# A two-group encoder layer on one core: the order of TensorE and SP in the two attention stages written out by hand, transposes placed between wide products, the scaling of P moved to GpSimd

## The chip, the cores and the metric

The kernel runs on one core of a Trainium2 chip. The metric is the device time of one execution in microseconds (us). Lower is better. TensorE (PE in the views) multiplies, VectorE (DVE), ScalarE (ACT) and GpSimd (POOL) do elementwise work, and SyncE (SP) issues most of the loads from the chip's main memory (HBM). Each engine has its own queue of instructions, fixed when the kernel is built, and waits on semaphores.

## The reference

One encoder layer is applied with the same weights to two groups of tokens: a prompt of 512 and a sample of 1024, both 1024 channels wide, everything in float32. Cut to what matters:

```
u    = layer_norm(x) * (1 + sc1) + sh1          # sh, sc, g from silu(c) @ w_ada
qa, ka, va, qb, kb, vb, ga, gb = split(u @ w_in)
qa, ka = rope(rms_norm(qa)), rope(rms_norm(ka))
oa   = softmax(qa ka' / 8) va                   # global attention, 8 heads, 2 kv heads
ob   = softmax(qb kb' / 8 + bias) vb            # 8 heads, each token sees a window of 8 x 16 tokens
m    = (sigmoid(ga) * (oa @ w_out_a) + sigmoid(gb) * (ob @ w_out_b)) @ w_out
x    = layer_norm_affine(2**0.25 * x + (1 + g1) * m)
h    = square(relu((layer_norm(x) * (1 + sc2) + sh2) @ w_ff1)) @ w_ff2
y    = layer_norm_affine(2**0.25 * x + (1 + g2) * h)
```

## The kernel before

Tokens are handled in chunks of 512: the prompt is one, the sample two. A large product is made three times, with each operand split into a high part in the fast 32-bit format (fp32r) and the low rest (`whi` and `wlo` for weights): `mm3` issues high x high, high x low, low x high. Weights come in units of 128 x 1024 values: SP loads a unit into `wraw` (three buffers), ACT writes `whi` (L93), DVE `wlo` (L94), and `stream` does that one unit ahead of its use. A unit feeds 24 products 512 columns wide for a chunk.

The stages, with the times at which the trace shows them: the modulation and the prompt's projections (`proj`, to about 187 us), the prompt's gates (to 285), the prompt's attention together with the projections of both sample chunks (285 to 640), the sample's attention together with the sample's gates and then the prompt's merge (640 to 1138), the merges, output product and norms of the three chunks (to 1436), and the dense layers (to the end). In `proj` the order is q, then k and v of the global attention, then q and k of the local one, then its v.

An attention stage has a global part `gqa` and a local part `na`. In `gqa` a block is a kv head, a head and 512 queries; the prompt has 8 blocks, the sample 16. A step of a block is one tile of 128 queries: score products S of the tile with all keys (L534: two products for 512 keys, four for 1024), the maximum on DVE (L537), the exponential on ACT (L540), a reciprocal (L541), and the scaling of P, on ACT and DVE in turn (L543, L545). The values of the block before go on meanwhile: for each 128 keys four transposes of P into a PSUM tile T (L552), a split of T into `ph` and `pl` (L555, L556), and two products with V into the sums A (L565, L566). Scores have two PSUM buffers of one bank in the prompt, one of two banks in the sample. In `na` an item is a head, eight rows of the image and 16 columns, 32 items in the prompt and 64 in the sample: two score products over a window of 256 or 384 keys (L657), bias and maximum in one DVE instruction (L660), exponential (L664), scaling on DVE (L666), two or three transposes (L673), a copy on ACT (L675), and two or three value products (L680). `load` brings V of a pair of heads in 16 pieces (L619), then Q and K of the head (L622, L108), one head ahead; the bias tables come separately (L635).

What fills PE between the attention's steps is the other generator of the stage. `weave` runs generators side by side: each yields a number for its progress, and the one that is least far goes on. This gives a program order; a planner then orders the instructions of every engine anew by its own estimates of their times and by priority, SP's loads among them. The sample's merge (`out_merge`) loads gates (`og`), multiplies them with the products of oa and ob, adds the two on GpSimd (L755), and splits the sum.

```
        self.weave(attention(0), self.chain(*[(self.proj(c, U, tmp), 1) for c, U in zip(scs, US)]), finish())
...
        self.weave(attention(1), fill())
```

## Time and profile before

| | |
|---|---|
| median of 3 runs | 2508.99 us (2502.77 to 2511.89) |
| the profiled execution's own time | 2521.03 us |
| its span, first to last instruction | 2519.2 us |
| PE, matmuls | 2391.9 us busy, 95% of the span |
| PE, weight loads | 1902.1 us, 76% |
| DVE | 1475.1 us, 59% |
| ACT | 972.3 us, 39% |
| GpSimd | 472.6 us, 19% |
| mean granted clock of PE | 0.975 of 2.4 GHz |

The profile is of one execution. Matmuls are pipelined: a record begins before the one ahead of it has ended, so a busy PE is not PE at its peak, and the distance between the starts of two products says more than their lengths. The granted clock is the share of full speed that the chip allowed PE; its two levels are 1.2 and 2.4 GHz. The rows on which the prediction rests are in a section of their own, below.

### The profile page before, as it was taken

The page shows a single profiled execution, that of the slowest core. Times are in us where ns is not written, and L with a number is a line of the kernel's source. Part 1 is how long each engine was busy: PE and PEld are TensorE (multiplying, and loading weights), DVE is VectorE, ACT ScalarE, POOL GpSimd, SP SyncE. Part 2 cuts the span into 40 slices and gives each one's busy share as a digit, 9 for nine tenths or more (in the row PEclk, how much of TensorE's full clock was granted, in tenths as well). Part 3 has the DMA queues.
Part 4 walks back from the last instruction along what each step waited for, and adds up shares of the span by engine and source line. Part 5 has one row for each costly group of instructions (what it writes and reads, how often), then busy time and mean ns, then how long its engine had stood idle before and what let it go on. Part 6 is the DMA issues. An engine that isn't in the chain of part 4 may idle for free.

```text
span 2519.2 us, 29833 instructions
## 1 busy us (share of the span) xinstructions
PE 2391.9 (95%) x10992; PEld 1902.1 (76%) x10992; DVE 1475.1 (59%) x2511; ACT 972.3 (39%) x1589; POOL 472.6 (19%) x524
## 2 busy tenths in 40 slices
PE   5989999988999999999897999999999999999997
PEld 3867777766777777777776788887788888888876
DVE  6997686474677754675867754445733333333466
ACT  4434656434677754553434224232411211221222
POOL 4341242353000004431312000003100000000133
PEclk9999999988999999999998999999999999999999
DMA  6766634576112127766656524234511210211231
GB/s 248 251 222 221 213 130 155 144 196 217 63 53 76 49 69 198 183 188 195 194 199 206 169 76 154 96 97 127 177 34 42 67 42 26 67 50 34 68 117 59
DMA packets 124227, 325.85 MB, mean 129 GB/s; under 512 B 20240, under 2 KB 35632, under 8 KB 124080
## 3 DMA queue, kind: packets, MB, share of 16 engines
q1 hardware_dynamic: 105744, 266.21, 34.8%
q0 software_dynamic: 18048, 57.69, 6.5%
q8 instruction: 87, 1.43, 0.2%
q14 instruction: 60, 0.49, 0.1%
q10 hardware_dynamic: 288, 0.03, 0.0%
HBM read 261.99 MB, written 62.93 MB: 129 GB/s over the span
## 4 chain that ended last, share of the span: by engine, by line
PE 66%; DVE 11%; issue 8%; DMA 7%; POOL 4%; ACT 2%; SPq 0%; POOLq 0%; ACTq 0%; DVEq 0%
PE D L112 18%; PE D L114 18%; PE D L113 18%; PE S L534 3%; PE T L552 3%; PE A L680 2%; DVE wlo L94 2%; PE A L565 2%; PE A L566 1%; DMA wraw<-in_wst 1%; PE T L673 1%; POOL og L755 1%; PE S L657 1%; ACT whi L93 1%; DMA og<-g 1%
## 5 line engine op out<-in xcount | busy, mean ns | idle before, releaser
L93 ACT ACTIVATE whi<-wraw 128x1024 fp32r<-128x1024 f32 x266 | 279.1, 1056 | 846.2 <-PE D L114 423.8
L114 PE MATMUL D<-uh,wlo 128*128 128x512 f32 x1344 | 534.1, 397 | 10.2 <-DVE wlo L94 10.2
L112 PE MATMUL D<-uh,whi 128*128 128x512 f32 x1344 | 536.0, 399 | 3.9 <-DVE stk L341 1.9
L113 PE MATMUL D<-ul,whi 128*128 128x512 f32 x1344 | 532.7, 396 | 0.0
L94 DVE TENSOR_TENSOR wlo<-wraw,whi 128x1024 fp32r<-128x1024 f32 x266 | 333.1, 1255 | 317.8 <-ACT whi L93 316.9
L112 PE MATMUL D<-whi,hh 128*128 128x512 f32 x768 | 304.6, 398 | 7.5 <-ACT hh L863 7.5
L114 PEld LDWEIGHTS D<-uh,wlo 128*128 128x128 f32 x1344 | 255.3, 190 | 68.6 <-DVE wlo L94 13.1
L114 PE MATMUL D<-whi,hl 128*128 128x512 f32 x768 | 303.6, 397 | 0.7 <-DVE hl L864 0.6
L113 PE MATMUL D<-wlo,hh 128*128 128x512 f32 x768 | 303.3, 397 | 0.0
L112 PEld LDWEIGHTS D<-uh,whi 128*128 128x128 f32 x1344 | 255.5, 190 | 59.2 <-issue 3.0
L113 PEld LDWEIGHTS D<-ul,whi 128*128 128x128 f32 x1344 | 255.5, 190 | 53.7 <-issue 0.9
L885 DVE TENSOR_TENSOR y<-y,D 128x512 f32<-128x512 f32 x168 | 115.2, 686 | 214.6 <-PE D L114 214.0
L112 PEld LDWEIGHTS D<-whi,hh 128*128 128x128 f32 x768 | 145.4, 189 | 44.7 <-ACT hh L863 11.2
L114 PEld LDWEIGHTS D<-whi,hl 128*128 128x128 f32 x768 | 145.3, 190 | 36.9 <-DVE hl L864 3.1
L113 PEld LDWEIGHTS D<-wlo,hh 128*128 128x128 f32 x768 | 145.5, 189 | 33.6
L846 POOL TENSOR_TENSOR y<-y,g 128x1024 f32<-128x1024 f32 x12 | 28.8, 2400 | 754.0 <-DVE y L885 754.0
L537 DVE TENSOR_REDUCE m<-S 128x1 f32<-128x1024 f32 (+1 forms) x96 | 99.7, 1041 | 44.8 <-PE S L534 44.6
L112 PE MATMUL D<-whi,uh 128*128 128x512 f32 (+1 forms) x288 | 106.0, 370 | 13.9 <-DVE stk L341 8.2
L556 DVE TENSOR_TENSOR pl<-T,ph 128x512 fp32r<-128x512 f32 x160 | 107.0, 684 | 14.6 <-ACT ph L555 13.8
L555 ACT ACTIVATE ph<-T 128x512 fp32r<-128x512 f32 x160 | 93.4, 596 | 52.2 <-PE T L552 50.7
L113 PE MATMUL D<-wlo,uh 128*128 128x512 f32 (+1 forms) x288 | 105.5, 366 | 3.1 <-DVE wlo L94 3.0
L114 PE MATMUL D<-whi,ul 128*128 128x512 f32 (+1 forms) x288 | 105.0, 365 | 0.0
(170 smaller groups left out, 3845.7 us busy)
## 6 DMA issues: line engine op xcount, KB each, us to landing
wraw<-in_w SPq DMA_DIRECT2D x132, 512.0 KB
wraw<-in_wst SPq DMA_DIRECT2D x56, 512.0 KB
wraw<-in_wada SPq DMA_DIRECT2D x32, 512.0 KB
g<-gst POOLq DMA_DIRECT2D x48, 256.0 KB, 3.5
og<-g SPq DMA_DIRECT2D x48, 256.0 KB
wraw<-in_wab SPq DMA_DIRECT2D x24, 512.0 KB
wraw<-in_wo SPq DMA_DIRECT2D x24, 512.0 KB
raw<-in_wada_k SPq DMA_DIRECT2D x16, 512.0 KB
```

Of the source, the lines that this page charges most:

```text
L93: nc.scalar.activation(hi, raw, AF.Copy)
L94: (engine or nc.vector).tensor_tensor(lo, raw, hi, op=ALU.subtract)
L112: mm(out, l[0], r[0], start=start, stop=False)
L113: mm(out, l[0], r[1], start=False, stop=False)
L114: mm(out, l[1], r[0], start=False, stop=stop)
L534: nc.tensor.matmul(S[:, k * CH:(k + 1) * CH], q, K[r][:, k * CH:(k + 1) * CH], start=r == 0, stop=r == 1)
L537: nc.vector.tensor_reduce(m, S[:, :T], axis=AX.X, op=ALU.max, negate=True)
L552: nc.tensor.transpose(tp[:, qt * P:(qt + 1) * P], Ps[qt][:, k * P:(k + 1) * P], self.ident)
L555: nc.scalar.activation(ph, tp, AF.Copy)
L556: nc.vector.tensor_tensor(pl, tp, ph, op=ALU.subtract)
L565: nc.tensor.matmul(acc, V[:, k, :], ph, start=k == 0, stop=False)
L885: nc.vector.tensor_tensor(y[:, hs], y[:, hs], ps, op=ALU.add)
```

## The change

In the two attention stages PE's and SP's instructions keep the order in which the program issues them (`in_order`), so `weave` alone sets it; the other engines stay with the planner, and softmax, splits and the ends of blocks are issued at high priority. For that every generator goes on in small steps. `mm3s` yields after each product, and takes a waiting transpose of a projection (`small`) behind each. `gqa` issues a transpose and a wide product in turn, its transposes two steps (prompt: one) after the block's last softmax, its value products two groups (one) later. `na` runs transposes two items behind the scores and value products three behind. Each part lets the other generator lead at first (`LEAD`, `NLEAD`).

P is scaled on GpSimd for three tiles of a block and on ACT for the fourth. In the sample's `gqa` scores have two PSUM buffers of two banks and the fill one bank (`psD1`), with eight empty yields after each gate chunk (`GAP`); `na` gives the fill a second bank. K of `gqa` has two buffers. Weights of the sample's projections and of the gates are asked for two units ahead. `proj` makes the local v first and does its ropes and stacks in the eight units of the local q and k; the rows of gates (`mod_finish`) come in the middle of the first sample chunk, and their store goes to GpSimd's queue. In `out_merge` of the sample the low part of the weights is made on GpSimd and the two gated products are added on DVE. The diff, cut:

```diff
-GL = 0.06
 AHEAD = 1
-GQ = (0.55, 0.55)
-AT = (1.1, 0.94)
+GQ = (0.55, 0.66)
+AT = (1.02, 0.96)
+LEAD = (0.06, 0.12)
+NLEAD = (0.2, 0.26)
+GAP = 8
+HP = 1000
...
+    def in_order(self, *gens):
+
+        with self.tc.manual_schedule(engines={mybir.EngineType.PE, mybir.EngineType.SP}):
+            self.weave(*gens)
...
+    def mm3s(self, out, l, r, start, stop):
+
+        mm = self.nc.tensor.matmul
+        for i, (x, y) in enumerate(((l[0], r[0]), (l[0], r[1]), (l[1], r[0]))):
+            mm(out, x, y, start=start and i == 0, stop=stop and i == 2)
+            if self.small:
+                self.small.pop(0)()
+            yield
...
-        return self.psD.tile([P, CH], F32, tag="D", name="D")
+        self.nd += 1
+        return self.psD[self.nd % len(self.psD)].tile([P, CH], F32, tag="D", name="D")
...
+                self.small.extend([lambda: None] * 10 + [partial(row, s, gi, c0)])
...
+        self.small.extend(partial(turn, t) for t in range(TT))
...
+    def proj_weights(self, chunks):
+        a = self.a
+        return self.stream(([a["wvb"][i] for i in range(4)] + [a["wq"][i] for i in range(4)]
+                            + [a["wkv"][i] for i in range(2)] + [a["wst"][i] for i in range(8)]) * chunks,
+                           ahead=chunks)
...
-        todo = {2: [(q_rope, 0)], 3: [(q_rope, 1), (k_rope, 0)], 4: [(q_rope, 2), (k_rope, 1)],
-                5: [(q_rope, 3), (k_rope, 2)], 6: [(k_rope, 3)],
-                7: [(q_stack, 0)], 8: [(q_stack, 1)], 9: [(q_stack, 2)], 10: [(q_stack, 3)], 11: [(k_stack, 0)]}
+        todo = {1: [(q_rope, 0), (k_rope, 0)], 2: [(q_rope, 1), (k_rope, 1)], 3: [(q_rope, 2), (k_rope, 2)],
+                4: [(q_rope, 3), (k_rope, 3)], 5: [(k_stack, 0), (q_stack, 0)], 6: [(q_stack, 1), (q_stack, 2)],
+                7: [(q_stack, 3)]}
...
-            for (seq, t0), p in zip(chs, ps):
+        for i, w in enumerate(self.stream([a["wst"][8 + i] for i in range(16)], ahead=2)):
+            for (seq, t0), U in zip(chs, Us):
+                ps = []
+                yield from self.wstats(w, U, ps)
                 g = pool.tile([P, CH], F32, tag="gst", name="gst", bufs=2)
-                nc.scalar.activation(g, p, func)
+                nc.scalar.activation(g, ps[0], func)
                 nc.gpsimd.dma_start(self.scr[seq]["g"][i][:, t0:t0 + CH], g)
+                for _ in range(GAP if len(self.psD) == 1 else 0):
+                    yield
...
+        LAG, DEPTH = (2, 2) if nh > 1 else (1, 1)
...
+                    got.append(psp.tile([P, T], F32, tag="ST" if nh == 1 else "S", name="S", bufs=3 if nh == 1 else 2))
+                nc.tensor.matmul(got[0][:, k * CH:(k + 1) * CH], q, K[r][:, k * CH:(k + 1) * CH],
+                                 start=r == 0, stop=r == 1)
...
+                p = pool.tile([P, T], F32, tag="P", name="P", bufs=8 + LAG)
+                z = pool.tile([P, 1], F32, tag="z", name="z", bufs=4)
+                nc.scalar.activation(p, S[:, :T], AF.Exp, bias=m, scale=1.0, accum_out=z)
+                nc.vector.reciprocal(z, z)
+                if qt < TT - 1:
+                    nc.gpsimd.tensor_scalar(p, p, z, None, op0=ALU.mult)
+                else:
+                    nc.scalar.activation(p, p, AF.Copy, scale=z)
+                Ps[blk].append(p)
...
-            if qt % 2:
-                nc.vector.tensor_scalar(p, p, z, None, op0=ALU.mult)
-            else:
-                nc.scalar.activation(p, p, AF.Copy, scale=z)
...
+            return [partial(turn, qt) for qt in range(TT)], split
...
+        second = [None] * (TT + LAG) + [(b, k) for b in blocks for k in range(nk)]
+        second[:TT + LAG] = [None] * (kq * (TT + LAG))
+        steps = len(second) // kq + 1
...
+            for j in range(kq):
+                small, split = [], None
+                if kq * i + j < len(second) and second[kq * i + j]:
+                    small, split = turns(*second[kq * i + j])
+                big, end = bigs[j * 2:j * 2 + 2], None
+
+                hold = DEPTH + (pend[0][1] == 0) if pend else 0
+                n = len(pend) - DEPTH + 1 if small else 2
+                while pend and n > 0 and (len(pend) >= hold or not small):
+                    b, e = products()
+                    big, end, n = big + b, end or e, n - 1
+                for n in range(max(len(small), len(big))):
+                    for x in (small, big):
+                        if n < len(x):
+                            x[n]()
+                    yield lead + (1.0 - lead) * (i + (j + (n + 1.0) / TT) / kq) / (steps + 1)
+                with self.tc.high_priority(HP):
+                    if split:
+                        split()
+                    if end:
+                        finish(end)
+            if softmax:
+                with self.tc.high_priority(HP):
+                    softmax()
+        while pend:
...
+        lead = NLEAD[seq]
+        yield lead
+        n = len(items)
+        for i in range(n + 3):
...
+            big, softmax = scores(*items[i]) if i < n else ([], None)
+            small, copy = turns(ps.pop(0)) if 2 <= i < n + 2 else ([], None)
+            for j in range(max(len(big), len(small))):
+                for x in (big, small):
+                    if j < len(x):
+                        x[j]()
+                with self.tc.high_priority(HP):
+                    if softmax and j == 1:
+                        ps.append(softmax())
+                    if copy and j == ng - 1:
+                        pts.append(copy())
+                yield lead + (1.0 - lead) * (i + (j + 1.0) / (1 + ng)) / (n + 3)
+            if i >= 3:
+                it, pt = items[i - 3], pts.pop(0)
+                for g in range(ng):
+                    weigh(*it, pt, g)
+                yield lead + (1.0 - lead) * (i + 1.0) / (n + 3)
...
+        ws = self.primed(self.stream((a["wab"][n] for n in range(KT)), engine=nc.gpsimd if seq else nc.vector))
...
-            nc.gpsimd.tensor_tensor(ts[0], ts[0], ts[1], op=ALU.add)
+            (nc.vector if seq else nc.gpsimd).tensor_tensor(ts[0], ts[0], ts[1], op=ALU.add)
...
+                if seq and name == "g":
+                    p, more = psum("psDn", bufs=1)
+                    self.psD = self.psD + [p]
...
+        ws = self.proj_weights(2)
+        both = [(self.share(self.proj(c, U, tmp, ws, f), 488), 1)
+                for c, U, f in zip(scs, US, (partial(self.mod_finish, tmp), None))]
+        self.in_order(self.chain(*both), attention(0))
...
-        self.psD, psD_st = psum("psD3", bufs=3)
+        p, psD_st = psum("psD1", bufs=1)
+        self.psD = [p]
...
-            for x in self.gates(scs, US, tmp, AF.Copy):
+            for x in self.share(self.gates(scs, US, tmp, AF.Copy), 768 + 16):
...
-
-        self.weave(attention(1), fill())
+            merge = self.share(self.out_merge(pc, om["pool"], M), 200)
+            next(merge)
+            yield 0.86
+            for x in merge:
+                yield 0.86 + 0.14 * x
+
+        self.in_order(fill(), attention(1))
         psD_st.close()
```

## Rows read from the trace of the kernel before

**Rows 1.** Busy time by stage: us, engines (x instructions), clock, DMA share, GB/s.

```profile
285.00:478.00 193.00, 184.66 (x941) 150.06 (x941) 129.99 (x235) 113.16 (x216) 73.83 (x93) 0.98 0.45 141
478.00:640.00 162.00, 140.62 (x612) 104.19 (x613) 86.07 (x239) 60.01 (x140) 61.31 (x90) 0.85 0.66 195
640.00:931.00 291.00, 290.69 (x1471) 226.09 (x1469) 209.07 (x312) 210.13 (x331) 18.87 (x34) 1.00 0.18 55
931.00:1138.00 207.00, 200.88 (x1084) 153.57 (x1082) 118.29 (x374) 96.55 (x228) 82.59 (x97) 0.98 0.70 185
1138.00:1436.00 298.00, 276.07 (x1168) 220.41 (x1167) 206.13 (x294) 108.02 (x144) 57.26 (x50) 0.96 0.59 192
```

**Rows 2.** Timeline of PE, sample's gqa: start us, us, engine, line, operation.

```profile
706.62 0.39 PE L566 MATMUL A<-pl,V 128*128 128x512 f32 x1
706.85 0.27 PE L552 MATMUL T<-ident,P 128*128 128x128 f32 x1
706.88 1.18 PE L534 MATMUL S<-K,Q 128*128 128x512 f32 x4
707.89 0.49 PE L552 MATMUL T<-ident,P 128*128 128x128 f32 x3
...
708.45 0.39 PE L566 MATMUL A<-pl,V 128*128 128x512 f32 x1
708.69 0.60 PE L552 MATMUL T<-ident,P 128*128 128x128 f32 x4
709.07 0.49 PE L565 MATMUL A<-ph,V 128*128 128x512 f32 x1
709.41 0.39 PE L113 MATMUL D<-ul,whi 128*128 128x512 f32 x1
```

**Rows 3.** Timeline of PE in the sample's na.

```profile
1005.12 0.87 PE L680 MATMUL A<-pt,V 128*64 128x128 f32 x6
1005.92 0.55 PE L673 MATMUL T<-ident,P 128*128 128x128 f32 x3
```

**Rows 4.** Waits of PE, 478 to 640: us in total, times, longest.

```profile
PE D L112 <- DVE stk L341: 6.5, 1, 6.5
PE S L657 <- DMA K<-kb: 5.8, 2, 4.0
PE S L657 <- DVE m L660: 5.6, 4, 2.1
```

**Rows 5.** Timeline of SP's issues, na of prompt and sample.

```profile
481.11 16.06 SPq L619 DMA_DIRECT2D V<-vb  x16
...
497.83 3.05 SPq L108 DMA_DIRECT2D K<-kb  x4
...
954.13 24.83 SPq L619 DMA_DIRECT2D V<-vb  x16
```

**Rows 6.** Groups by line and form: busy us, mean ns, idle before.

```profile
L537 DVE TENSOR_REDUCE m<-S 128x1 f32<-128x1024 f32 x64 | 78.0, 1219 | 25.4 <-PE S L534 25.4
...
L540 ACT ACTIVATE P<-S,m 128x1024 f32<-128x1024 f32 x64 | 71.4, 1115 | 14.6 <-DVE m L537 13.9
...
L545 ACT ACTIVATE P<-P,z 128x1024 f32<-128x1024 f32 x32 | 36.7, 1148 | 4.3 <-DVE z L541 4.3
...
L846 POOL TENSOR_TENSOR y<-y,g 128x1024 f32<-128x1024 f32 x12 | 28.8, 2400 | 754.0 <-DVE y L885 754.0
...
L497 ACT ACTIVATE gst<-D 128x512 f32<-128x512 f32 x48 | 28.3, 589 | 44.3 <-PE D L114 24.7 <-DMA g<-gst 10.9 <-issue 8.6
...
L543 DVE TENSOR_SCALAR P<-P,z 128x1024 f32<-128x1024 f32 x32 | 24.1, 754 | 1.1
...
L94 POOL TENSOR_TENSOR wlo<-raw,whi 128x1024 fp32r<-128x1024 f32 x8 | 20.2, 2526 | 18.6 <-ACT whi L93 15.9 <-PE D L231 2.6
```

**Rows 7.** Waits of PE, 1138 to 1436: us in total, times, longest.

```profile
PE D L114 <- DVE wlo L94: 10.8, 4, 4.7
```

**Rows 8.** Line L94: operation, count, ns min/median/max, first and last start.

```profile
L94 DVE TENSOR_TENSOR wlo<-wraw,whi x266: 1166/1225/3343, 42.6 to 2476.3; 128x1024 fp32r<-128x1024 f32 x133
```

More of the change, by code (lines that the diff above doesn't have):

```diff
@@ new lines, in scores, with turns, turn, split @@
+            return [partial(product, k, r) for k in range(nh) for r in range(2)], softmax
+        def turns(blk, k):
+            got = []
+            def turn(qt):
+                if not got:
+                    got.append(psp.tile([P, CH], F32, tag="ST" if nh == 1 else "T", name="T", bufs=3 if nh == 1 else 2))
+                nc.tensor.transpose(got[0][:, qt * P:(qt + 1) * P], Ps[blk][qt][:, k * P:(k + 1) * P], self.ident)
+            def split():
+                tp = got[0]
+                ph = pool.tile([P, CH], F32R, tag="ph", name="ph", bufs=2 + DEPTH)
+                pl = pool.tile([P, CH], F32R, tag="pl", name="pl", bufs=2 + DEPTH)
+                nc.scalar.activation(ph, tp, AF.Copy)
+                nc.vector.tensor_tensor(pl, tp, ph, op=ALU.subtract)
+                pend.append((blk, k, ph, pl))
+            return [partial(turn, qt) for qt in range(TT)], split
@@ L570, in finish, with products, product @@
+        def products():
+            blk, k, ph, pl = pend.pop(0)
+            V = KV[blk[0]][1]
+            def product(i, p):
+                if k == 0 and i == 0:
+                    acc[blk] = psp.tile([P, CH], F32, tag="A", name="A", bufs=1)
+                nc.tensor.matmul(acc[blk], V[:, k, :], p, start=k == 0 and i == 0, stop=k == nk - 1 and i == 1)
+            return [partial(product, 0, ph), partial(product, 1, pl)], (blk if k == nk - 1 else None)
+        def finish(blk):
             kv, h, qc = blk
+            a = acc.pop(blk)
@@ new lines, in gqa @@
+        yield lead
+        kq = nk // TT
+        first = [(b, qt) for b in blocks for qt in range(TT)]
+        second = [None] * (TT + LAG) + [(b, k) for b in blocks for k in range(nk)]
+        second[:TT + LAG] = [None] * (kq * (TT + LAG))
+        steps = len(second) // kq + 1
+        for i in range(steps):
+            bigs, softmax = [], None
+            if i < len(first):
+                blk, qt = first[i]
+                if qt == 1:
+                    n = i // TT
+                    if n + 1 < len(blocks):
+                        load(blocks[n + 1][0], blocks[n + 1][1])
+                    if n + nh < len(blocks):
+                        load(None, blocks[n + nh][1])
+                bigs, softmax = scores(blk, qt)
+            for j in range(kq):
[21 more added lines that the diff above has]
+                    softmax()
@@ L597, in na @@
+        while pend:
+            big, end = products()
+            for x in big:
+                x()
+                yield 1.0
+            if end:
+                finish(end)
     def na(self, seq, pool, psp):
@@ L648, in bias, with scores @@
             biases[h, rt, b] = wm
-        def softmax(h, rt, b):
+        def scores(h, rt, b):
             Q, K = load(h)
@@ new lines, in scores, with turns, turn, copy @@
+            return [partial(product, r) for r in range(2)], softmax
+        def turns(p):
+            got = []
+            def turn(g):
+                if not got:
+                    got.append(psp.tile([P, NK], F32, tag="T" if nrt > 1 else "ST", name="T", bufs=2 if nrt > 1 else 3))
+                nc.tensor.transpose(got[0][:, g * P:(g + 1) * P], p[:, g * P:(g + 1) * P], self.ident)
+            def copy():
+                pt = pool.tile([P, NK], F32, tag="pt", name="pt", bufs=3)
+                nc.scalar.activation(pt, got[0], AF.Copy)
+                return pt
+            return [partial(turn, g) for g in range(ng)], copy
```

304 lines of the change are left out of this document (142 added, 162 removed).

## The prediction

> **What bounds the kernel now.** The stage table comes first [rows 1]. The reader is to see that TensorE (PE) is busy for 1092.9 of the 1151 us in these five stretches (184.7 + 140.6 + 290.7 + 200.9 + 276.1), so that only two things can shorten them: idle time of PE, and time in which its clock is at the lower of its two levels. The prompt's attention is the bad place: its neighbourhood part (NA, 478 to 640 us) has 21.4 us of idle PE and a mean clock of 0.85, so about 30% of 162 us, 49 us, at 1.2 GHz, where a product takes twice as long, which costs up to 24 us more. The sample's global attention (640 to 931) shows 0.3 us idle at clock 1.00.
>
> A busy PE can hide a stall inside a product's record, so I count products too, with prices from PE's own timeline. A product 512 columns wide starts 0.23 us after the one before (706.62 to 706.85) [rows 2]. A transpose costs 0.11 to 0.13 us more: from 706.62 to 707.89 there are five wide products and one transpose, 1.27 - 5 x 0.23 = 0.12; from 708.45 to 709.41 two wide ones and four transposes in a row, 0.96 - 0.46 = 0.50, so 0.125 each. In NA the value products of an item leave two narrow records each, and six records take 0.80 us with the turn to the next kind, 0.13 each [rows 3]. Products of 256 and 384 columns I take in proportion, 0.12 and 0.17.
>
> With the counts of records in [rows 1], split by what the code issues in each stretch: 285 to 478 has 192 projection products of 256 columns, 148 transposes (128 of P, 20 of q and k) and 601 wide ones, 23.0 + 16.3 + 138.2 = 177.5 us of 193, excess 15. 478 to 640 has 64 scores, 128 value records, 84 transposes and 336 wide, 7.7 + 16.6 + 9.2 + 77.3 = 110.8 of 162, excess 51. 640 to 931 has 512 transposes and 959 wide, 56.3 + 220.6 = 276.9 of 291, excess 14. 931 to 1138 has 378 value records, 194 transposes, 128 scores of 384 columns and 384 wide, 49.1 + 21.3 + 21.8 + 88.3 = 180.5 of 207, excess 26. These 106 us are all that a better order of the two attention stages can win; their products stay the same.
>
> Which wait ends last in NA of the prompt: PE's list is short and mixed, a stack that frees a PSUM bank 6.5 us, loads of K 5.8, score maxima 5.6 [rows 4]. No engine is full (DVE 86 of 162, ACT 60, GpSimd 61 in [rows 1]); the order is at fault, since attention steps wait on their own softmax while projection products that need nothing stand later in PE's queue.
>
> **The change part by part.** *The weave.* After it every attention product stands between fill products at a fixed rate, transposes of a block come one or two steps after its last softmax, and value products one or two groups later. In the sample's global attention a step is one softmax tile; 64 of them in 291 us make 4.5 us a step. The chain from scores to scaled P is 1.22 (maximum) + 1.12 (exp) + 1.15 (scale on ACT) = 3.5 us, with the reads of sums and the reciprocal near 4 [rows 6]; the lag of two steps, 9 us, covers it. In the prompt one step of 193 / 32 = 6 us covers a chain of half the width. So the idle time and the low clock that softmax causes should go.
>
> *Transposes between wide products.* Worth nothing by themselves: 0.12 for a lone one against 0.125 in a row of four [rows 2]. Bounds: 896 transposes of P by 0.015 us, 13 us either way; I take 0.
>
> *P on GpSimd.* It takes 32 scalings of 1024 columns off DVE (0.75 us each) and 16 of 32 off ACT (1.15 each), and gives GpSimd 48. GpSimd's price isn't shown; below it is DVE's 0.75, above GpSimd's two-input row of 2.40 [rows 6]. I take 2.4, as the engine is the same. Three of a block's four tiles go there; the third still has three steps, 13.5 us, before its transposes, against 1.22 + 1.12 + 2.4, about 5. GpSimd is busy for 19 of 291 us there [rows 1]; 48 x 2.4 = 115 more fit. Cost 0 while that lead lasts.
>
> *One PSUM bank for the fill, two for the scores.* In the sample's global attention a gate chunk must be evicted (0.59 us on ACT [rows 6]) before the next may start, about 0.9 us with the way there and back by my estimate. The eight empty yields between chunks let eight attention pairs of 0.12 + 0.23 us pass, 2.8 us, which hides it. In the fill-only lead before attention starts there are about four chunk ends with no cover: 4 us lost. The second score buffer takes away small waits of the order of the 14 us excess; I take 7 of it.
>
> *SP's order.* This part speaks against the change. NA loads V in 16 pieces per head pair, ahead of Q and K; the piece train took 16.06 us in the prompt and 24.83 in the sample, then Q and, in 3.05 us, K [rows 5]. Written out by hand, a weight load that comes after such a train in program order waits behind it. Weights are now asked for two units ahead; a unit of 24 wide products is 5.5 us alone and about 8 us woven. At the start of NA in the prompt PE has fill only (up to progress 0.2 of NA), the train with Q, K and bias is 16.1 + 3.1 and a little, about 20 us, and I estimate 6 more for landing and splitting: 26 us, against 2 to 3 units, 11 to 16 us. I charge 10 us there and 8 for the three later trains, 18 in all; below it is 0 (SP runs ahead), above the rival's price. In the sample a gate unit feeds two chunks, 11 us, so two units cover 22.
>
> *Sums.* Prompt attention: excess 15 + 51 = 66; I leave 8 in the global part, 18 for trains and 8 for the drain of the last items: gain 32. Sample attention: 14 to 7 plus the 4 lost at the start, a gain of 3; NA 26 to 15, a gain of 11 (the train still takes 25 us of a head pair's 50): 14.
>
> *The merge of the sample chunks.* In 1138 to 1436 PE idles 21.9 us [rows 1] and waits 10.8 us for weight splits (wlo) on a DVE that other work keeps, 4 times [rows 7]. The change gives these splits to GpSimd (2.53 us against DVE's 1.2 [rows 6, 8]), which is busy 57 of 298 us, and takes the add of the gated halves from it to DVE. A split of 2.53 fits in a unit of 24 products, 5.5 us. Gain between 0 and 10.8; I take 8.
>
> *The rest.* The order of the prompt's projections (value first), finer steps in gates and modulation, weight lookahead of two in the gates, the gate rows (mod_finish) later and their store on GpSimd's queue: DVE has the same work, 0, within 5 us either way.
>
> Sum: 32 + 14 + 8 = 54. The profiled execution took 2521.0 us (span 2519.2 and 1.8 around it), so 2467 by its own measure; the median of the runs shown, 2509.0, lies 12.0 lower, and with the same distance the forecast is **2455 us**. About 0.5%, 12.5 us, is what a measurement here can tell from no change.
>
> **The rivals.** *Nearly all of it comes back.* If trains hide behind SP's lead, prompt attention keeps 15 of 66 and the sample 15 of 40; 51 + 25 + 8 = 84, 2425 us. For it: no engine is full in these stages. Against it: the trains.
>
> *The stalls change place.* DVE, ACT and GpSimd stay in the planner's order; if it puts weight splits ahead of the softmax that PE's fixed queue needs next, NA keeps its 51 and 26 and the trains' 18 come on top of the 10 + 3 + 8 won elsewhere: 2506, no change. For it: the largest waits in [rows 4] end on DVE and on loads, whose order stays the planner's or moves to SP's list.
>
> *SP is the bound of NA; the kernel is slower.* One mechanism: every train stops the weights and the next head's K. If each of the 8 trains (four a sequence) leaves PE short by 15 us (26 less 11) once, by 10 us three times, and by 9 us four times in the sample (31 less 22), that is 81 us, and each stop of that size brings some 7 us at the lower clock, 3.4 us more: 108 in place of the 18 charged. 2455 + 90 = 2545. It decides from 54 / 8 = 6.8 us a train above what is charged. For it: 16 to 25 us trains, SP with K behind V [rows 5]. Against: the same trains are in the kernel before, and loads of K cost PE 5.8 us there [rows 4].
>
> *GpSimd holds up DVE.* DVE's split, 1.2 us at the median, at the longest took 3.3 [rows 8]; GpSimd's new work may do that more often. If all 115 us of the new scalings stopped DVE, the sample's global attention would have 209 - 24 + 115 = 300 us of DVE in 291 us [rows 1], DVE-bound: the 3 us won there go and 9 are lost, 2467. The Trainium skill (SBUF — State Buffer, section "SBUF: two separate sides") says that DVE and GpSimd share a pair of ports, held by one of them for a whole instruction; by its wording only DVE operations with two SBUF inputs, or in a two-port mode, are held. The stretched split agrees with it; by that reading the score maximum and the split of P, which read PSUM, would go on, and this rival is the weak end of the rule.
>
> **How the numbers follow.** Forecast 0.55, nearly all 0.11, the stalls change place 0.13, SP the bound 0.16, DVE held 0.05. Forecast, nearly all and DVE held are faster by over 0.5%, less a little of the forecast's spread: 0.70; same 0.14; slower 0.16. The likeliest case alone spans 2430 to 2485. The range goes from 2422 (leaving out some 0.07 below) to 2522 (taking in the middle case and the milder half of SP's, leaving out 0.11).
>
> **What would show it.** Right: in NA of the prompt PE's idle time falls from 21 us to under 10 and the clock from 0.85 to 0.95 or more; the sample's NA ends its excess at 15 or less; waits for wlo in the merge vanish. The prompt's attention stage is then some 32 us shorter, the sample's 14. Wrong: PE waits for K loads or for whi behind V trains (SP), for P from GpSimd, or the low clock shows at the start of each NA part.

## The result, and the profile after

The changed kernel takes 2540.84 us (median of 4 runs, 2538.27 to 2546.75) against 2509.72 us (median of 4 of the kernel before): ratio 1.0137, 95% interval 1.0121 to 1.0154. It is 1.4% slower; the forecast was 2455 us, and the range ended at 2522.

The profiled execution took 2546.75 us (span 2545.0), 25.8 us of span more than the one before. Four marks of the timeline cut both spans: the starts of the first score product of the prompt's global attention, of the last value product of its neighbourhood attention, of the last product of the prompt's merge, and of the first relu of the feed-forward part. Before they lie at 285.1, 622.1, 1149.2 and 1422.1 us, after at 285.1, 605.5, 1166.8 and 1445.5. So the prompt's attention is 16.6 us shorter, the sample's attention with the prompt's merge 34.2 longer, the rest of the output stage 5.8 longer, and the feed-forward part 2.4 longer.

The first two of these stretches as wholes, in the form of [rows 1] (engines in the order PE, its weight loads, DVE, ACT, GpSimd), two lines of before and two of after:

```profile
285.10:622.10 337.00, 307.31 (x1476) 239.75 (x1476) 212.98 (x470) 170.40 (x352) 132.94 (x178) 0.92 0.54 165
622.10:1149.20 527.10, 520.67 (x2681) 402.91 (x2679) 335.67 (x694) 311.75 (x566) 108.38 (x137) 0.99 0.41 113
...
285.10:605.50 320.40, 295.03 (x1481) 229.51 (x1479) 206.25 (x450) 160.80 (x340) 164.72 (x192) 0.97 0.55 160
605.50:1166.80 561.30, 525.21 (x2692) 395.48 (x2690) 324.42 (x668) 298.08 (x555) 242.44 (x190) 0.98 0.39 116
```

In the prompt's stage PE's idle time fell from 29.7 to 25.4 us and the mean clock rose from 0.92 to 0.97: most of the 16.6 us came with the clock. In the sample's stage the idle time rose from 6.4 to 36.1 us, which is nearly all of the 34.2.

Busy time of three stages of the changed kernel, as [rows 1] of before, cut where they now lie:

```profile
478.00:606.00 128.00, 113.35 (x614) 85.54 (x613) 89.77 (x249) 62.06 (x152) 61.29 (x78) 0.99 0.63 178
...
622.00:889.00 267.00, 251.08 (x1298) 190.72 (x1297) 176.91 (x262) 177.84 (x292) 149.25 (x76) 0.99 0.16 53
...
1103.00:1167.00 64.00, 54.58 (x206) 39.52 (x205) 31.73 (x40) 19.42 (x26) 11.22 (x9) 0.92 0.70 225
```

The first row is the prompt's neighbourhood attention: the clock is 0.99 where it was 0.85, as forecast, but PE still idles 14.7 us, where the forecast had it fall from 21 to under 10. The second is the sample's global attention: PE idles 15.9 of 267 us, where it idled 0.3 of 291, though DVE and ACT are busy for 66 and 67% of it (72% each before). The third is new: 64 us in which the prompt's merge stands almost alone (12 attention products are left in it), with 9.4 us idle at clock 0.92.

Waits of PE in the changed kernel, in the prompt's neighbourhood attention [rows 4], the sample's global attention, the lone merge, and the output stage [rows 7] (us in total, times, longest):

```profile
PE T L811 <- DVE P L800: 6.4, 4, 2.9
...
PE T L641 <- DVE pl L648: 10.4, 11, 1.9
PE A L661 <- DVE o L671: 2.5, 2, 1.8
PE T L641 <- POOL P L628: 1.4, 1, 1.4
...
PE D L142 <- DVE og L908: 5.4, 3, 2.2
...
PE D L134 <- ACT whi L115: 12.5, 3, 5.9
...
PE D L142 <- POOL wlo L116: 6.6, 6, 1.5
```

The waits for wlo in the output stage, which by the forecast were to vanish, are 6.6 us (10.8 before), and 12.5 us of waits for whi come on top (0.8 before). The largest wait of the global attention is none that the prediction priced. A transpose (T) needs a PSUM bank, and its bank is free only when DVE has taken the low half (pl) of an older block out of it. Timeline of all engines around one such wait, as far as it bears on it (in brackets how long the engine idled before, and what ended it):

```profile
656.43 0.60 ACT L572 ACTIVATE gst<-D 128x512 f32<-128x512 f32 x1 [0.48 <-PE D L142]
...
656.92 0.59 ACT L647 ACTIVATE ph<-T 128x512 fp32r<-128x512 f32 x1
...
657.47 1.23 DVE L622 TENSOR_REDUCE m<-S 128x1 f32<-128x1024 f32 x1 [1.32 <-PE S L616]
657.61 0.27 PE L641 MATMUL T<-ident,P 128*128 128x128 f32 x1
657.63 0.47 PE L661 MATMUL A<-pl,V 128*128 128x512 f32 x1
...
658.61 1.28 DVE L648 TENSOR_TENSOR pl<-T,ph 128x512 fp32r<-128x512 f32 x2
...
659.43 0.30 PE L641 MATMUL T<-ident,P 128*128 128x128 f32 x1 [1.33 <-DVE pl L648]
```

ACT evicts a gate chunk first, so ph starts at 656.92 and ends at 657.51; DVE has by then begun the maximum of the next scores, 1.23 us, and pl starts at 658.61. The next transpose stands still until 659.43, and with it the products behind it in PE's fixed order: a score product at 659.49, the first fill product at 660.72.

### The profile page after: what moved, and what is told of

It is laid out like the page before. It is cut to its first block, busy times and chain, and to the rows that moved or that the text cites. A ratio compares the mean times of both kernels' runs of the same rounds, so it can differ in the third digit from the quotient of the medians.

```text
span 2545.0 us, 30057 instructions
## 1 busy us (share of the span) xinstructions
PE 2380.3 (94%) x10992; PEld 1879.1 (74%) x10992; DVE 1458.4 (57%) x2463; ACT 950.2 (37%) x1565; POOL 655.0 (26%) x600
## 4 chain that ended last, share of the span: by engine, by line
PE 60%; DVE 11%; issue 9%; DMA 9%; ACT 4%; POOL 4%; SPq 0%; POOLq 0%; ACTq 0%; DVEq 0%
PE D L134 13%; PE D L136 13%; PE D L135 13%; PE D L142 11%; DMA wraw<-in_wst 4%; DVE wlo L116 2%; PE S L616 2%; PE A L823 2%; PE A L661 2%; PE T L641 2%; ACT whi L115 2%; DVE junk L291 1%; PE S L789 1%; PE T L811 1%; POOL wlo L116 1%
## 5 line engine op out<-in xcount | busy, mean ns | idle before, releaser
L116 DVE TENSOR_TENSOR wlo<-wraw,whi 128x1024 fp32r<-128x1024 f32 x250 | 318.4, 1277 | 352.0 <-ACT whi L115 351.3
L136 PE MATMUL D<-uh,wlo 128*128 128x512 f32 x768 | 301.7, 393 | 6.6 <-DVE wlo L116 6.6
L134 PE MATMUL D<-uh,whi 128*128 128x512 f32 x768 | 301.8, 393 | 1.1 <-ACT whi L115 1.1
L135 PE MATMUL D<-ul,whi 128*128 128x512 f32 x768 | 301.3, 392 | 0.0
L142 PE MATMUL D<-uh,whi 128*128 128x512 f32 x576 | 241.7, 420 | 3.9 <-ACT whi L115 2.4
L142 PE MATMUL D<-uh,wlo 128*128 128x512 f32 x576 | 241.2, 419 | 2.2 <-DVE wlo L116 2.2
L142 PE MATMUL D<-ul,whi 128*128 128x512 f32 x576 | 241.9, 420 | 0.0
L628 POOL TENSOR_SCALAR P<-P,z 128x1024 f32<-128x1024 f32 (+1 forms) x72 | 176.3, 2451 | 129.5 <-DVE z L626 85.3
L641 PE MATMUL T<-ident,P 128*128 128x128 f32 x640 | 173.2, 275 | 13.2 <-DVE pl L648 11.4
L136 PEld LDWEIGHTS D<-uh,wlo 128*128 128x128 f32 x768 | 144.5, 188 | 40.4 <-DVE wlo L116 8.4
L134 PEld LDWEIGHTS D<-uh,whi 128*128 128x128 f32 x768 | 144.6, 188 | 33.8 <-ACT whi L115 2.0
L135 PEld LDWEIGHTS D<-ul,whi 128*128 128x128 f32 x768 | 144.6, 188 | 32.0
L616 PE MATMUL S<-K,Q 128*128 128x512 f32 x320 | 144.1, 473 | 7.0 <-ACT P L625 5.9
```

The costliest lines, as they stand in the source:

```text
L116: (engine or nc.vector).tensor_tensor(lo, raw, hi, op=ALU.subtract)
L134: mm(out, l[0], r[0], start=start, stop=False)
L135: mm(out, l[0], r[1], start=False, stop=False)
L136: mm(out, l[1], r[0], start=False, stop=stop)
L142: mm(out, x, y, start=start and i == 0, stop=stop and i == 2)
L616: nc.tensor.matmul(got[0][:, k * CH:(k + 1) * CH], q, K[r][:, k * CH:(k + 1) * CH], start=r == 0, stop=r == 1)
```

## The experiments

Twelve further kernels ran, each of them the whole layer. Ratios are to the kernel before, measured on the same chip along with it. Where two of these kernels are compared "by the ratio", their ratios are divided. Stage lengths are by the four marks, of one profiled execution each, which lies up to 7 us off its kernel's median: the five other kernels with the prompt's order by hand throughout spread over 321.0 to 325.2 us in the prompt's attention, so a few us mean nothing there.

| kernel | ratio [95%] | prompt attention | sample attention, merge | output | feed-forward |
|---|---|---|---|---|---|
| before | 1 | 337.0 | 527.1 | 272.9 | 1097.1 |
| changed | 1.0137 [1.0121, 1.0154] | 320.4 | 561.3 | 278.7 | 1099.5 |
| e1_pace | 1.0207 [1.0184, 1.0231] | 325.0 | 573.2 | 276.9 | 1095.1 |
| e2_p_alt | 1.0212 [1.0189, 1.0234] | 325.2 | 568.7 | 278.7 | 1097.0 |
| e3_planner_sample | 1.0081 [1.0059, 1.0103] | 323.6 | 538.4 | 278.0 | 1094.4 |
| e4_planner_prompt | 1.0097 [1.0074, 1.0119] | 314.1 | 557.7 | 280.3 | 1098.8 |
| e5_merge_before | 1.0130 [1.0112, 1.0149] | 323.1 | 560.7 | 269.0 | 1096.3 |
| e6_pe_only | 1.0106 [1.0088, 1.0124] | 317.8 | 560.2 | 278.1 | 1098.3 |
| e7_planner_both | 1.0021 [1.0006, 1.0036] | 315.2 | 540.2 | 277.6 | 1093.8 |
| e8_tail | 1.0119 [1.0099, 1.0139] | 321.0 | 552.0 | 274.8 | 1099.5 |
| e9_combined | 0.9947 [0.9929, 0.9965] | 313.3 | 530.7 | 267.4 | 1095.8 |
| e10_combined_pace | 0.9937 [0.9921, 0.9954] | 312.9 | 526.7 | 271.2 | 1096.4 |
| e11_combined_p_alt | 0.9941 [0.9924, 0.9958] | 311.5 | 530.3 | 270.6 | 1096.7 |
| e12_before_p_gpsimd | 1.0121 [1.0099, 1.0144] | 344.9 | 539.5 | 276.6 | 1096.9 |

**The pace of the gates.**

```diff
-            for x in self.share(self.gates(scs, US, tmp, AF.Copy), 768 + 16):
+            for x in self.share(self.gates(scs, US, tmp, AF.Copy), 768 + 16 + 152):
```

> Theory A (pace): the gates of the sample are handed out as if they had 784 steps, but the empty steps between chunks make some 936 of them, so the gates end together with the neighbourhood attention (last eviction at 1103 us), and the prompt's merge then runs with nothing woven between; that tail lost 14 us against the kernel before. With the true count the gates should end near 80% of the stage, the merge should run beside the last attention items, and the kernel should be 10 to 15 us faster than the changed one: about 2526 to 2531 us. Rival B (feed): the merge has one PSUM bank and three load buffers, and is slow beside anything; then its waits only move forward, and the time stays within 5 us of 2541. Rival C (fixed order in the global attention): the steps there get more fill, so the waits for the split of the transposed P shrink too; then the gain is larger than 15 us.

2558.56 us, 0.7% slower than the changed kernel: theory A failed. The gates end at 1038 us instead of 1103, and the merge does run beside attention from 1065 us on, but the stage as a whole is 11.9 us longer. One wait is as long, in SP's, DVE's and PE's timelines of this run:

```profile
1066.63 16.30 SPq L748 DMA_DIRECT2D V<-vb  x16
...
1086.87 0.93 SPq L905 DMA_DIRECT2D og<-g  x2
...
1098.20 1.33 DVE L908 TENSOR_TENSOR og<-D,og 128x512 f32<-128x512 f32 x2 [9.04 <-DMA og<-g]
...
1098.94 0.79 PE L142 MATMUL D<-oh,whi 128*128 128x512 f32 x1 [11.97 <-DVE og L908]
```

The fill has two PSUM banks at that point, and both hold finished products of the merge. They come free when DVE multiplies them with gate tiles (two in a row from 1098.20); the loads of these tiles stand in SP's written order behind a train of 16 V pieces and the loads of Q, K and bias after it, are issued at 1086.87, and end the wait 11 us later. In these 11 us the DMA engines were busy throughout (from 1084 to 1098 us a share of 1.00, 224 GB/s), so the loads issued just ahead have a part in the wait beside SP's order; the run doesn't divide it between the two. PE's written order lets nothing pass, and 12 us go. The forecast's rival on SP's trains is real here, once; rival B, with its one bank and three buffers, named another resource.

**P as before.**

```diff
-                if qt < TT - 1:
-                    nc.gpsimd.tensor_scalar(p, p, z, None, op0=ALU.mult)
+                if qt % 2:
+                    nc.vector.tensor_scalar(p, p, z, None, op0=ALU.mult)
```

> P is scaled as in the kernel before, odd tiles on DVE and even ones on ACT, all else as in the changed kernel. Theory A (DVE is late): PE waits in the sample's global attention for DVE's split of the transposed P, which stands behind 1.22 us of score maximum; 32 scalings of 0.75 us more on DVE and 16 of 1.15 us more on ACT there make these waits worse, 5 to 15 us slower than the changed kernel. Rival B (GpSimd is late or holds up the others): the 72 scalings of 2.85 us at the median are what the steps wait for; then the time falls by 5 us or more. Rival C (the lag covers it): no change within 5 us, which would make the move to GpSimd worth nothing either way.

2559.97 us, 0.74% slower than the changed kernel by the ratio: theory A, with a loss of 19 us, over its 15. The wait for pl in the sample's global attention grows from 10.4 to 17.0 us:

```profile
PE T L641 <- DVE pl L648: 17.0, 20, 2.3
```

In the fixed order the relief of DVE and ACT by GpSimd is worth 19 us; the longer waits for pl account for 6.6 of them, the rest isn't traced to one wait.

**The planner's order in one stage.** In the first of these two kernels the sample's attention is woven without the fixed order, in the second the prompt's:

```diff
-        self.in_order(fill(), attention(1))
+        self.weave(fill(), attention(1))
```

```diff
-        self.in_order(self.chain(*both), attention(0))
+        self.weave(self.chain(*both), attention(0))
```

> The sample's attention with TensorE's and SP's order from the planner again, the prompt's by hand; the functions stay as changed. Theory A (the hand order of this stage is the loss): the stage and the prompt's merge give back their 28 us, about 2513 us, near the kernel before. Rival B (the loss lies in what is emitted, that is the pace of the gates, the one fill bank and the lags): the planner can't repair it, and the time stays within 8 us of 2541. Rival C: the planner is worse with functions that are written for a fixed order (lags of two steps, two banks for T and S), over 2549 us.

> The prompt's attention with TensorE's and SP's order from the planner again, the sample's by hand. Theory A (the hand order won what the two traces show there): the low clock comes back in the prompt's neighbourhood part (mean 0.97 by hand, 0.85 before) and the time rises by about 10 us, to 2551. Rival B (the new functions won it, whoever orders them): within 5 us of 2541, clock above 0.93. Rival C (SP's order costs something at the start of the stage that the planner saves): faster by 5 us or more.

Sample by the planner: 2527.47 us, half of theory A's gain by the ratio (0.56%, 14 us). Its global attention takes 255 us, 12 less than the changed kernel's, and none of PE's waits in it is for pl. Prompt by the planner: 2531.59 us, a gain of 0.40%, 10 us, which none expected but rival C. The prompt's stage, 314 us, is shorter than by hand: what shortened it against the kernel before is the new functions with their lags, not the order by hand. Theory A's low clock didn't come back: 0.94 on the mean from 478 to 600 us.

**The hand order on PE alone.**

```diff
-        with self.tc.manual_schedule(engines={mybir.EngineType.PE, mybir.EngineType.SP}):
+        with self.tc.manual_schedule(engines={mybir.EngineType.PE}):
```

> TensorE's order stays written by hand in both attention stages, SP's goes back to the planner. Theory A (SP's fixed order is the loss: loads behind the V trains): waits for K, weights and gate loads shrink, and the kernel is 10 us or more faster than the changed one, 2530 us or less. Rival B (TensorE's fixed order is the loss: it stands at the first late softmax or split although other products are ready): no change within 5 us. Rival C (a list that the planner makes for SP without an order for TensorE to follow is worse): slower by 5 us or more.

2533.14 us, 0.31% (8 us) off: between A and B. By stage it is clear for the sample, where nothing changed (560.2 us against 561.3) and the wait for pl stayed:

```profile
PE T L641 <- DVE pl L648: 11.5, 11, 2.6
```

There PE's order is the loss. In the prompt 317.8 us lies between hand (320 to 325) and planner (312 to 315), so there SP's order may have a part.

**The planner's order in both stages** (both edits of above).

> Both attention stages with the planner's order, the rest as changed. The runs with one stage so gave 13 us (sample) and 9 us (prompt) against the changed kernel. Theory A (the two are independent): 22 us together, about 2518 us, still 0.4% above the kernel before. Rival B (they share a cause, such as the place where one stage hands over to the next): 13 to 16 us, 2525 us or more. Rival C: the planner recovers all, 2509 us or less, and then nothing but the hand order was wrong with the change.

2514.07 us, ratio 1.0021: theory A, with 29 us by the ratio instead of 22. Busy time of its global attention in the sample, and the first and last of PE's four kinds of waits there:

```profile
615.00:869.00 254.00, 252.24 (x1309) 194.96 (x1310) 174.35 (x262) 176.38 (x292) 149.41 (x76) 0.99 0.20 60
```

```profile
PE S L616 <- issue: 3.3, 1, 3.3
...
PE T L641 <- POOL P L628: 0.2, 1, 0.2
```

With the same instructions on the same engines PE idles 1.8 us instead of 15.9, and this part takes 254 us instead of 267. That the planner has fill products in the place where the hand has a transpose that isn't ready is the likely reading; the two orders were not laid side by side.

**The merge of the sample's chunks as before.**

```diff
-        ws = self.primed(self.stream((a["wab"][n] for n in range(KT)), engine=nc.gpsimd if seq else nc.vector))
+        ws = self.primed(self.stream((a["wab"][n] for n in range(KT))))
...
-            (nc.vector if seq else nc.gpsimd).tensor_tensor(ts[0], ts[0], ts[1], op=ALU.add)
+            nc.gpsimd.tensor_tensor(ts[0], ts[0], ts[1], op=ALU.add)
```

> Only the merge of the sample's chunks goes back: weight splits on DVE, the add of the gated halves on GpSimd. Theory A (the split on GpSimd is too slow for the products that follow it): the six waits of 6.6 us on GpSimd and part of the waits of 12.5 us on the ACT half of a split go, and the stretch from the prompt's merge to the feed-forward part, 278.7 us in the changed kernel and 272.9 before, falls by about 6 us: 2535 us. Rival B (as predicted, the old assignment is the worse one): the waits for wlo on DVE come back and the time rises by 5 to 10 us. Rival C (the new waits come from the finer steps or the lookahead of the streams): no change within 3 us.

2540.05 us: by the ratio 0.07% less, which the intervals can't tell from nothing, so by the time alone it is rival C. By its profile the output stage falls by 9.7 us, to 269.0, and the table bears that out: the eight kernels with this part of the change have 274.8 to 280.3 us there, the four with it put back 267.4 to 271.2. So theory A stands; the add goes back together with the split, and no run parts the two. Its waits for splits are 9.9 us where they were 19.1 (12.5 and 6.6) in the changed kernel:

```profile
PE D L142 <- DVE wlo L116: 5.2, 4, 2.0
PE D L134 <- ACT whi L115: 4.7, 3, 2.8
```

Where the 12.5 us come from is seen in the longest wait of the changed kernel, on GpSimd's, SP's, ACT's and PE's timelines:

```profile
1190.21 2.41 POOL L116 TENSOR_TENSOR wlo<-wraw,whi 128x1024 fp32r<-128x1024 f32 x1 [4.51 <-ACT whi L115]
...
1192.71 0.64 ACT L892 ACTIVATE oh<-wraw 128x512 fp32r<-128x512 f32 x1 [2.01 <-DMA wraw<-ob]
...
1196.90 4.01 SPq L110 DMA_DIRECT2D wraw<-in_wo  x3
...
1201.36 1.06 ACT L115 ACTIVATE whi<-wraw 128x1024 fp32r<-128x1024 f32 x1 [1.73 <-DMA wraw<-in_wo]
...
1202.47 2.08 PE L134 MATMUL D<-whi,mh 128*128 128x512 f32 x4 [5.76 <-ACT whi L115]
```

All weights and attention outputs go through three raw buffers (wraw). A split that takes 2.4 us on GpSimd holds one of them twice as long as DVE's 1.2; in the timeline the attention outputs come some 2 us after ACT is ready for them, and the weights of the next products queue up behind these loads. By this reading, which no run tested by itself, the price lies with the next load, not with the products that use the split.

**Two banks for the prompt's merge.** The bank that the fill gets for the neighbourhood attention is kept until the merge has ended:

```diff
             if more:
-                self.psD = self.psD[:1]
-                more.close()
+                self.more = more
...
         self.in_order(fill(), attention(1))
+        self.more.close()
         psD_st.close()
```

> The second fill bank, given back when the sample's neighbourhood attention ends, is kept until the prompt's merge has ended; so the merge has two banks. Theory A (the tail of the prompt's merge, 61.9 us with 18.7 us beyond what its products need, is set by the eviction of its one bank, 5.4 us of waits and a low clock): 6 to 12 us faster, 2529 to 2535 us. Rival B (it is set by loads of the merge's inputs and weights, 0.3 to 2 us each): within 4 us of 2541. As the run with the true pace showed, a merge that stands beside the attention items isn't hidden either.

2537.17 us: 0.18%, 4.5 us by the ratio, with intervals that overlap, so the time doesn't decide between the theories; by its profile it is theory A, for the merge's products take 53.0 us instead of 61.9, and the wait for the bank falls from 5.4 us to 1.3:

```profile
PE D L142 <- DVE og L908: 1.3, 2, 0.7
```

**The combination**: planner in both stages, merge as before, two banks.

> The planner's order in both attention stages, the second fill bank kept through the prompt's merge, and the merge of the sample's chunks as before. Theory A (the three are separate losses): 2514 less 4.5 for the bank (ratios 1.0137 and 1.0119) and less 2 to 9 for the merge (median and stage of its run), 2500 to 2508 us, ratio 0.997 to 0.999: what stays of the change is then a gain of less than 0.5%. Rival B (the planner already fills the merge's tail and stage): 2511 to 2517.

> The combined kernel, and the gates handed out by their true count, so that they end before the attention does and the prompt's merge runs beside the last neighbourhood items, as in the kernel before. By hand this cost 17 us, with a wait of 12 us for a product that one bank and a gate load behind SP's V train held. Theory A (that loss was SP's order and the single bank): with the planner and two banks it is gone, within 4 us of the combined kernel or up to 10 us faster. Rival B (the gates are simply the better fill for the neighbourhood items, the merge a poor one): 8 us or more slower than the combined kernel.

> The combined kernel with P scaled as before (odd tiles on DVE, even ones on ACT). By hand this cost 19 us, and waits for DVE's split of P rose from 10.7 to 17.0 us. Theory A (DVE's load matters only where TensorE may not go past the late product): with the planner's order the scaling's place is worth under 5 us. Rival B (DVE's load is the loss in itself): 10 to 19 us slower than the combined kernel.

2495.49 us, ratio 0.9947 (0.9929 to 0.9965): faster than the kernel before by 13 us (by the ratio), and than the one with the planner alone by 0.74%, 19 us, more than either theory gave. The lone merge (59.3 to 50.1 us) and the output stage (277.6 to 267.4) account for 19.4. With the true pace 0.9937, with P as before 0.9941: neither can be told from it. The pace's 17 us and the 19 us of the scaling's place thus don't belong to the work; they come with the hand order, for the pace perhaps with the single bank, which went back at the same time.

Busy time of the combined kernel in the prompt's neighbourhood attention, the sample's global attention and the prompt's merge, to be held against the three rows of the changed one:

```profile
478.00:597.00 119.00, 105.74 (x578) 80.50 (x579) 89.00 (x241) 61.31 (x151) 60.15 (x77) 0.97 0.67 195
...
612.00:866.00 254.00, 251.90 (x1308) 194.62 (x1308) 174.31 (x261) 176.13 (x292) 149.03 (x75) 0.99 0.20 60
...
1077.00:1127.00 50.00, 47.07 (x190) 36.10 (x191) 32.83 (x40) 17.47 (x23) 11.73 (x8) 0.97 0.81 272
```

PE idles 13.3, 2.1 and 2.9 us there, against 14.7, 15.9 and 9.4. The sample's attention with the prompt's merge, as a whole:

```profile
596.30:1127.00 530.70, 518.40 (x2693) 395.96 (x2691) 325.42 (x667) 296.48 (x555) 244.07 (x190) 0.99 0.41 121
```

It idles 12.3 us, where the kernel before idled 6.4, and is 3.6 us longer.

**P on GpSimd alone**, in the kernel before, without the longer lead:

```diff
-            if qt % 2:
-                nc.vector.tensor_scalar(p, p, z, None, op0=ALU.mult)
+            if qt < TT - 1:
+                nc.gpsimd.tensor_scalar(p, p, z, None, op0=ALU.mult)
```

> The kernel before with one part of the change alone: three of a block's four P tiles are scaled on GpSimd, the fourth on ACT, without the longer lead. Theory A (worth nothing without a fixed order): within 8 us of before. Rival B (the scaling of 2.85 us without a lead of two steps makes TensorE wait): 10 us or more slower, and then the lead is what makes the move possible. Rival C (DVE's and ACT's relief shows by itself): 8 us or more faster.

2538.86 us, 1.2% slower: rival B. The line of the scaling in this run (first its durations, ns min/median/max), and who waits for it:

```profile
L543 POOL TENSOR_SCALAR P<-P,z x72: 1555/2842/2852, 289.6 to 931.7; 128x1024 f32<-128x1024 f32 x48, 128x512 f32<-128x512 f32 x24
...
  PEld T L552: 27.2, 19
  PE T L552: 20.9, 15
```

PE waits 20.9 us for P. In the changed kernel, with a lag of two steps, it waits 1.4. By this comparison, in which other parts differ too, the lead is what makes the move possible; what the move then brings is nothing that can be told (e9_combined against e11_combined_p_alt).

## Why the prediction was wrong

**The prompt's attention (32 forecast).** The low clock went as forecast, 0.85 to 0.99, and the stage lost 16.6 us, half the term; 22 to 26 us with the planner's order. The direction was right, and half the size. What came is the clock's share; the idle time, which the term also counted on, fell by 4.3 us only (29.7 to 25.4). And the weave by hand isn't what wins it: e4_planner_prompt leaves PE and SP to the planner and is faster still, so the lags and the lead in which the new functions give out their work are enough. The 18 us charged for trains don't show: no wait of PE between 285 and 606 us of the changed kernel ends on a load, and one, of 1.7 us, on whi; the waits of the neighbourhood part end on softmax and copies (DVE and ACT). What the hand order costs in this stage is about 10 us (a mean of 323 us over six kernels against 313 over five), on SP and PE.

**The sample's attention (14 forecast): the step that failed.** It measured 34.2 us the other way. The text took the chain from scores to scaled P, 9 us of lead against 4 us, and concluded that "the idle time and the low clock that softmax causes should go". That chain does hold: P is late once, for 1.4 us. A second one wasn't costed: transpose, ph on ACT, pl on DVE, bank free, with two banks for T. ACT and DVE serve it between an exp, a gate eviction and a maximum of 1.2 us, in the order that the planner gave them, and PE stood still with fill behind it. e3_planner_sample and e7_planner_both take the order away and these waits are gone. By the ratios the hand order costs 14 us in the sample and 29 us in both stages; by the profiled stages 21 to 23 in the sample. The other piece is the one bank for the fill: the text charged it 4 us in the lead, and looked at the gates only. Its price is in the merge that comes after attention, 61.9 us against 53.0 with two banks.

With both put right the 14 us still don't come: 530.7 us in e9_combined and 526.7 in e10_combined_pace, against 527.1 before. The prediction's first paragraph says that "only two things can shorten them", idle time and low clock. Of these the sample's stage had 6.4 us and about 4 (rows 1 of before: 207 us at 0.98), 10 in all. The excess of 14 + 26 us by product prices is for the most part time in which PE was busy at the higher clock, and in no run was the stage more than 0.4 us shorter than before.

**Transposes between wide products (0 forecast)** is borne out. Timeline of PE in the changed kernel, as [rows 2] of before:

```profile
706.06 0.39 PE L142 MATMUL D<-ul,whi 128*128 128x512 f32 x1
706.29 0.27 PE L641 MATMUL T<-ident,P 128*128 128x128 f32 x1
706.32 0.47 PE L616 MATMUL S<-K,Q 128*128 128x512 f32 x1
706.63 0.39 PE L142 MATMUL D<-uh,wlo 128*128 128x512 f32 x1
```

From 706.06 to 706.63 there are two wide products and one lone transpose, 0.57 - 0.23 - 0.23 = 0.11 us for the transpose, next to 0.125 in a row.

**P on GpSimd (cost 0 while the lead lasts)** held, at a higher price than taken: 2.85 us each, above the upper bound of 2.40 from the two-input row [rows 6]. An engine's price for one operation was a poor bound for another.

**The merge of the sample chunks (8 forecast)** measured 5.8 us the other way, and some 8 us come back when it is undone (the two groups of kernels under e5_merge_before). The split was held against the products that use it; by the reading above, the raw buffer that it holds was overlooked.

**The rivals.** "The stalls change place" had the mechanism, DVE's order by the planner under a fixed queue on PE, but put it in the neighbourhood parts, and priced it as what is there already; it was the global part, and it costs more than nothing. (Its sum has "10 + 3 + 8 won elsewhere", where the text's own terms for the prompt's global part, 15 less 8, leave 7 in place of 10.) "SP is the bound" gave 2545, close to the result, by luck and the wrong cause: with SP back at the planner 8 us go, not 90, and in the sample none. "GpSimd holds up DVE" is refuted for the scaling of P: the split of P on DVE takes 689 ns on the mean against 684 before, the maximum 1220 against 1219, with GpSimd busy for 149 of 267 us. The Trainium skill (SBUF — State Buffer, section "SBUF: two separate sides") would hold only DVE's two-input SBUF work or two-port modes; that the PSUM reads go on beside GpSimd agrees with it. By the same wording the scaling of P could hold DVE's weight split, which has two SBUF inputs; here the measurement decides against that: of eleven such splits that overlap a scaling in the changed kernel, ten took 1.21 to 1.29 us and one 1.51. Beside GpSimd's own two-input split the hold is there, twice in the changed kernel's output stage, at 3.20 us. One of each kind (GpSimd's instruction, then DVE's):

```profile
305.53 1.57 POOL L628 TENSOR_SCALAR P<-P,z 128x512 f32<-128x512 f32 x1
306.15 1.22 DVE L116 TENSOR_TENSOR wlo<-wraw,whi 128x1024 fp32r<-128x1024 f32 x1 [0.70 <-ACT whi L115]
...
1249.56 2.38 POOL L116 TENSOR_TENSOR wlo<-wraw,whi 128x1024 fp32r<-128x1024 f32 x1
1249.83 3.20 DVE L116 TENSOR_TENSOR wlo<-wraw,whi 128x1024 fp32r<-128x1024 f32 x1
```

Open: how SP and PE share the 10 us of the prompt's hand order, and whether a fixed order on all of PE, SP, ACT and DVE would do what this one didn't; it wasn't tried.

## What to carry to other kernels

An order fixed by hand on one engine turns a late producer into a stop of that engine, so cost each buffer's way back (who frees it, in which order that engine works) and not only the way of the data forward. Here, where a planner orders the other engines, leaving it PE's order as well was better; writing the order of all of them was not tried. Before counting on an excess over product prices, hold it against idle time and low clock: in the sample's stage, where it was mostly neither, no order made the stage shorter. Before judging one part of a bundled change, undo the order with the rest kept: here the planner's order, a second PSUM bank kept and a merge put back make 1.4% slower into 0.5% faster.

## What was unexpected of the hardware

GpSimd takes longer for P by a column of 128 scalars (2.85 us for 128 x 1024, 1.56 for 128 x 512 at the least) than for adding two full tiles of that size (2.40 [rows 6]). And after a short stop more can go than the stop itself: in the three us before 699 PE of the changed kernel was busy for 1.20, with a wait of 1.80 us for o; the granted clock then was 0.57 for 3.9 us and back at 1.00 after it. At the lower of its two levels (1.2 of 2.4 GHz) for most of that stretch, PE loses some 1.7 us (3.9 x 0.43), about the length of the wait again. Not each such wait is followed by this: after one of 1.85 us that ended at 641.41 the granted clock was 1.00 (641.4 to 645 us).

The row of the wait, and the windows before, in and after the slow stretch:

```profile
698.59 0.50 PE L661 MATMUL A<-ph,V 128*128 128x512 f32 x1 [1.80 <-DVE o L671]
```

```profile
696.00:699.00 3.00, 1.20 (x8) 0.72 (x7) 2.44 (x4) 2.79 (x6) 2.55 (x1) 1.00 0.00 0
699.00:702.90 3.90, 3.90 (x14) 2.85 (x13) 0.99 (x3) 1.94 (x5) 1.37 (x3) 0.57 0.33 101
702.90:706.00 3.10, 3.10 (x17) 2.42 (x16) 1.92 (x2) 1.03 (x2) 0.00 (x0) 1.00 0.00 0
```
